# New places in memory for four operand tiles, and a new rank table, in a three-layer fp32 decoder kernel on one core

## The chip, the core and the metric

The kernel runs on one core of a Trainium2 chip as one launch. The metric is the device time of an execution in microseconds (us), as a median of several executions. The engines go by the profile's names: PE is TensorE (PEld its weight loads), DVE is VectorE, ACT is ScalarE, POOL is GpSimd, SP issues the DMAs.

## The reference, cut to what matters

Three transformer layers over 256 tokens of 1024 features, all in fp32: a layer of gated linear attention ("gla"), a layer of sparse attention ("nsa"), both with attention to a memory of 256 rows and a convolutional feed-forward block, and a layer with forgetting attention ("fox"), pooling and 16 meta tokens put ahead.

```python
x = first_block(x, mem, ...)      # for each of two layers:
    h = rmsnorm(x, g_mix[l])
    x = x + gla_layer_mix(h, ...)  or  nsa_layer_mix(h, shared, ...)
    x = x + conv_ffn(rmsnorm(x, g_ffn[l]), w_up[l], conv_w[l], conv_b[l], w_down[l])
return second_block(x, ...)       # _layer: forgetting attention + pooling, then silu(gate) * up, down
```

Nearly all arithmetic is in products of activations with weight matrices of 1024 rows (2816 for the three down projections).

## The kernel before

**Products in three passes.** Every weight piece `w` (128 x up to 1024 numbers) arrives in `wraw` by DMA and is split: ACT rounds it to `whi` (`_cuts`), and DVE subtracts, `wlo = wraw - whi` (`_rest`). Activations are split in the same way into a high and a low tile. A block of 128 output columns is then, for each 128 rows `kk` of the contraction, three matmuls with 128 x 128 stationary weights and 256 streamed columns (`mm3`, line 516 records them): `whi` with the high part, `whi` with the low part, `wlo` with the high part. In the profile's names the weights stand last: `acc<-xh,wlo`.

**Streamed operands.** There are three kinds: the sets `xh`/`xl` (two of them, each 8 x 272 numbers per partition) hold the normed input of a projection; `ch`/`cl` hold the heads' outputs ahead of an output projection; `hh`/`hl` hold the hidden layer ahead of a down projection. All lie in SBUF at addresses that the order of the `base.tile` calls sets. In the built program the pieces `whi` and `wlo` are multiples of 1024 bytes apart. Counted from them modulo 1024 bytes, `ch`, `cl`, `hh` and `hl` lie at 704, both `xl` at 704, and both `xh` at 192. One row `kk` of a streamed operand is 1024 bytes per partition (1088 where it holds 272 columns), one stationary block 512 bytes.

**Order of the work.** The program has no loop. Python generators (threads) yield operations, and `Sched.run` writes the operations out one by one: of the threads that are ready it takes the one with the lowest `cost + NEAR * rank`. The rank comes from the table `PRIO` by the generator's name; `RATIO` and `LIMIT` set a credit that decides when PE's small matmuls may go ahead of a main product. An operation written `V.op | G.op` goes to DVE or POOL, whichever the planner thinks will end it earlier. Engines run their own instructions strictly in the order written, and wait for each other by semaphores.

**The place that the change reorders most** is in the gla layer, for the second half (`tt == 1`) of the tokens. `expo` makes tables on ACT and DVE (`gqe`, `ge`, `gqx`); `levels` multiplies them on PE in groups (`att<-gqe,ge`, `att<-gq,gk`, `att<-gqx,gkx`); `near_pairs` copies each group out of PSUM with DVE (`near<-gc,att`, then `gat<-near` and `gat<-att`); `out_rows` multiplies the result with the values (`att<-gv,gat`, and `att<-gv,gax`). At the same time `mem_set` builds the set for the memory (`xl<-mem,vec,xh`), and `mm3` continues with the projection `mq`.

Of the kernel before, what the change touches and what calls it, by code (L numbers as in the profile page):

```python
# [6 lines left out]
FT = mybir.dt.float32  # L7
FR = mybir.dt.float32r
# [120 lines left out]
class Ev:  # L129


    def __init__(self):
        self.t = None
# [20 lines left out]
class Thread:  # L154
    def __init__(self, gen, prio, t, n):
# [2 lines left out]

LNEXP, EXPTANH, SILU = "natural_log_exp_and_others", "exp_and_others", "silu_and_others"
TABLES = {"Exp": (LNEXP, EXPTANH), "Ln": (LNEXP,), "Silu": (SILU,), "Tanh": (EXPTANH,)}  # L160
LOAD, TICK, RATIO, LIMIT, WARM, SWITCH = 1.3, 3.4133, 1.4792, 0.7664, 12, 0.13
NEAR = 0.00100

PRIO = {"_cuts": -18.58, "_load": 1.02, "_loads": -36.85, "_rest": -3.82, "add_residual": -13.55,
        "both_norms": -19.45, "ck_load": -13.23, "ck_loads": -83.76, "coefs": 59.38, "compress": -19.77,
        "consts": 24.44, "decay": -37.28, "evacuate": 6.42, "expo": -55.79, "few_loads": 48.21, "forget": -38.18,
        "fox_chain": -4.22, "fox_pair": 5.05, "proj_few": 10.05, "fox_head": 2.42, "gains": 32.58, "gate": 23.42,
        "gating": -11.27, "head_norm": -20.5, "heads_of": -2.08, "hidden": 7.95, "late_loads": -16.69,
        "levels": 7.47, "mem_chain": -63.57, "mem_head": -11.75, "meta_probs": 1.9, "meta_rows": 0.62,
        "meta_values": -15.47, "mix": -47.97, "near_pairs": -10.15, "nsa_chain": -4.61, "out_rows": -68.21,  # L170
        "output": -6.62, "pads": 18.74, "pooling": -11.72, "rows_done": 28.61, "rstd_rows": -52.41,
        "scale_few": -6.07, "scale_out": -25.81, "scale_tok": -70.73, "selection": 91.16, "silu": 15.66,
        "smalls": 30.82, "square_sum": -6.06, "squares": 39.11, "stack_k": -9.03, "stack_q": 22.34, "swap": 33.71,
        "tile_parts": -14.4, "up": -47.17, "values": -19.21, "warm": -9.83, ("square_sum", 3): 31.92,
        ("square_sum", 5): 13.26}
HOP = {"P": 0.24, "V": 0.14, "S": 0.16, "G": 0.29, "D": 0.24}


# [222 lines left out]
class Weights:  # L401


    def __init__(self, sch, plan, dram, dma, V, S, G, raw, hi, lo):
        self.sch, self.plan, self.dram, self.dma, self.V, self.S, self.G = sch, plan, dram, dma, V, S, G
# [47 lines left out]

    def _rest(self, p, raw, o, m, left):
        p.lo = yield self.lo
        parts = p.lo[:, :m], raw[:, o:o + m], p.hi[:, :m].bitcast(FT)
        yield self.V.tensor_sub(*parts) | self.G.tensor_sub(*parts)
        self.sch.set(p.ev)
        left[0] -= 1
        if not left[0]:  # L460
            self.sch.give(self.raw, raw)
# [21 lines left out]
def body(tc, io):  # L483
    from contextlib import ExitStack
    nc = tc.nc
    sch = Sched(nc)
    V, S, G = Eng("V", nc.vector), Eng("S", nc.scalar), Eng("G", nc.gpsimd)
# [7 lines left out]
    def slots(pl, n, shape, name, dt=FT):  # L495
        return Slots([pl.tile(shape, dt, name=f"{name}{i}") for i in range(n)])
# [27 lines left out]
    def tr(*calls):  # L524

        def fn():
            for o, a, b in calls:
# [8 lines left out]
    base = pool("base")  # L536
# [6 lines left out]
    W = Weights(sch, _plan(), io["w"], dma, V, S, G, slots(base, 2, [128, CHUNK], "wraw"),  # L543
                slots(base, NP, [128, PIECE], "whi", FR), slots(base, NP, [128, PIECE], "wlo", FR))
    rco = base.tile([128, 10], FT, name="rco")
    rsq = base.tile([128, 10], FT, name="rsq")
    minus_half = base.tile([128, 10], FT, name="mhalf")
    sets = Slots([(base.tile([128, KD, LT], FR, name=f"xh{i}"), base.tile([128, KD, LT], FR, name=f"xl{i}"))
                  for i in range(2)])
    x = base.tile([128, KD, T], FT, name="x")  # L550
    meta = base.tile([128, KD, META], FT, name="meta")
# [5 lines left out]
    tiny = Slots(tinys + [base.tile([128, 32], FT, name=f"tiny{i}") for i in range(2, 10)])  # L557
# [11 lines left out]
    def C(name):  # L569
        o, n = COFF[name]  # L570
        return cst[:, o:o + n]
# [6 lines left out]
        o, n = VOFF[name]  # L578
        return vec[:, o:o + n]

    ident, ones = C("ident"), base.tile([128, 128], FT, name="ones")


    def mm3(ps, b, st, cols=lambda a: a, first=True, last=True):
# [381 lines left out]
    def main():  # L966
# [25 lines left out]
        with ExitStack() as stack:  # L992
# [40 lines left out]
            alrT, qT, kT = t_([128, T], "alrT"), t_([128, 2, T], "gq"), t_([128, 2, T], "gk")  # L1033
# [43 lines left out]
            def expo(tt, f, out):  # L1077
                c = slice(tt * 128, tt * 128 + 128)
                yield la_ev, gr_ev
                et = yield e_  # L1080
                e = et.rearrange("p (a b) -> p a b", a=8)
                qe = yield qes
                for half in range(2):
                    bank = yield att
                    a0 = 128 * tt + 512 * half
                    yield pe(*[(bank, w[:, tt, f * 128:f * 128 + 128], gr[:, a0:a0 + 512], i == 0, i == 1)
                               for i, w in enumerate((lh, ll))])
                    yield S.activation(et[:, half * 512:half * 512 + 512], bank, AF.Exp, scale=1.0 / 16.0)
                    give(att, bank)
                yield q_ev[f], k_ev[f]  # L1090
                l0 = 1 - tt
                yield V.tensor_mul(qe, e[:, l0:l0 + 7], qT[:, f, None, c].to_broadcast([128, 7, 128]))
                ke = e[:, l0:l0 + 7]
                parts = ke, ke, kT[:, f, None, c].to_broadcast([128, 7, 128])
                yield V.tensor_mul(*parts) | G.tensor_mul(*parts)
                if tt == 0:
                    yield V.tensor_mul(kx[:, f, :], e[:, 0], kT[:, f, c])
                else:
                    yield V.tensor_mul(qx[:, f, :], e[:, 7], qT[:, f, c])
                kx_ev[tt, f] = Ev()  # L1100
                sch.set(kx_ev[tt, f])
                out.append((et, qe, ke))
# [458 lines left out]
        rm_ev, c = Ev(), {}  # L1561
# [514 lines left out]
```

## Time and profile before

| | |
|---|---|
| runs shown | 923.35, 929.02, 929.19 us; median 929.02 |
| profiled execution | 923.24 us, of which 921.5 us from the first to the last instruction |
| PE busy | 899.9 us, 7967 matmuls |
| DVE, ACT, POOL busy | 717.0, 493.2, 90.4 us |

PE's busy time counts a matmul from its start to a modelled end, so matmuls that follow each other overlap; how dense PE works is read from the number of matmuls in a stretch. Stages by the span's time: start to 24 us, gla to 101, its output projection to 150.7, first feed-forward block to 327.4, nsa to 420, output projection to 460.6, second feed-forward block to 638, fox to 718.5, output projection to 745, last feed-forward block to the end.

### The profile page before, as it was taken

The page shows a single profiled execution, that of the slowest core. Times are in us where ns is not written, and L with a number is a line of the kernel's source. Part 1 is how long each engine was busy: PE and PEld are TensorE (multiplying, and loading weights), DVE is VectorE, ACT ScalarE, POOL GpSimd, SP SyncE. Part 2 cuts the span into 40 slices and gives each one's busy share as a digit, 9 for nine tenths or more (in the row PEclk, how much of TensorE's full clock was granted, in tenths as well). Part 3 has the DMA queues.
Part 4 walks back from the last instruction along what each step waited for, and adds up shares of the span by engine and source line. Part 5 has one row for each costly group of instructions (what it writes and reads, how often), then busy time and mean ns, then how long its engine had stood idle before and what let it go on. Part 6 is the DMA issues. An engine that isn't in the chain of part 4 may idle for free.

```text
span 921.5 us, 19560 instructions
## 1 busy us (share of the span) xinstructions
PE 899.9 (98%) x7967; PEld 864.7 (94%) x7967; DVE 717.0 (78%) x1492; ACT 493.2 (54%) x854; POOL 90.4 (10%) x116
## 2 busy tenths in 40 slices
PE   8988999999999999999999999999999999999998
PEld 7877999999999996989999999999889999999998
DVE  7776588999987687986899999867688777777552
ACT  5644556555554544875565555545666554444431
POOL 3211001000000012300200000112352100000000
PEclk9977999999999999999999999999999999999999
DMA  7721535555555566233445555555323355555651
GB/s 268 265 70 70 183 138 169 198 183 193 200 202 184 190 239 238 90 138 96 180 184 186 200 206 188 184 186 206 131 93 128 127 182 205 185 187 194 217 209 64
DMA packets 26668, 160.19 MB, mean 174 GB/s; under 512 B 3242, under 2 KB 5674, under 8 KB 8530
## 3 DMA queue, kind: packets, MB, share of 16 engines
q1 hardware_dynamic: 26578, 158.94, 48.5%
q8 instruction: 63, 1.03, 0.4%
q14 instruction: 27, 0.22, 0.1%
HBM read 157.62 MB, written 1.05 MB: 172 GB/s over the span
## 4 chain that ended last, share of the span: by engine, by line
PE 86%; DVE 10%; DMA 2%; issue 1%; ACT 0%; SPq 0%; DVEq 0%; ACTq 0%
PE acc L516 76%; PE att L516 8%; DVE wlo L335 4%; PE att L528 2%; DVE xl L335 2%; DMA ck<-in_w_cv_dram 1%; DVE x L335 1%; DVE sum L335 1%; DMA ck<-in_w_ck_dram 1%; DMA mem<-in_w_dram 0%; DVE xh L335 0%; DVE gqx L335 0%; DVE ge L335 0%; DVE gqe L335 0%; DVE near L335 0%
## 5 line engine op out<-in xcount | busy, mean ns | idle before, releaser
L335 ACT CAST whi<-wraw 128x1024 fp32r<-128x1024 f32 x280 | 294.4, 1052 | 319.5 <-PE acc L516 305.0
L335 DVE TENSOR_TENSOR wlo<-wraw,whi 128x1024 fp32r<-128x1024 f32 x279 | 345.2, 1238 | 103.8 <-ACT whi L335 102.9
L516 PE MATMUL acc<-xh,whi 128*128 128x256 f32 (+1 forms) x1440 | 408.2, 283 | 0.1
L516 PE MATMUL acc<-xh,wlo 128*128 128x256 f32 (+1 forms) x1440 | 400.9, 278 | 2.0 <-DVE wlo L335 2.0
L516 PE MATMUL acc<-xl,whi 128*128 128x256 f32 (+1 forms) x1440 | 401.0, 278 | 1.4 <-DVE xl L335 1.3
L516 PEld LDWEIGHTS acc<-xh,whi 128*128 128x128 f32 x1440 | 271.4, 189 | 6.5 <-issue 4.2
L516 PEld LDWEIGHTS acc<-xl,whi 128*128 128x128 f32 x1440 | 271.9, 189 | 2.6 <-DVE xl L335 2.2
L516 PEld LDWEIGHTS acc<-xh,wlo 128*128 128x128 f32 x1440 | 271.4, 188 | 2.8 <-DVE wlo L335 2.8
L516 PE MATMUL acc<-hh,whi 128*128 128x256 f32 x528 | 146.0, 276 | 0.0
L516 PE MATMUL acc<-hl,whi 128*128 128x256 f32 x528 | 145.7, 276 | 0.0
L516 PE MATMUL acc<-hh,wlo 128*128 128x256 f32 x528 | 145.7, 276 | 0.0
L516 PEld LDWEIGHTS acc<-hh,whi 128*128 128x128 f32 x528 | 99.1, 188 | 0.0
L516 PEld LDWEIGHTS acc<-hl,whi 128*128 128x128 f32 x528 | 99.1, 188 | 0.0
L516 PEld LDWEIGHTS acc<-hh,wlo 128*128 128x128 f32 x528 | 99.1, 188 | 0.0
L335 POOL TENSOR_TENSOR sum<-sum,sqt 128x256 f32<-128x256 f32 x27 | 28.9, 1070 | 477.5 <-ACT sqt L335 469.0
L516 PE MATMUL acc<-ch,whi 128*128 128x256 f32 x192 | 55.3, 288 | 0.0
L516 PE MATMUL acc<-cl,whi 128*128 128x256 f32 x192 | 53.1, 277 | 0.0
L516 PE MATMUL acc<-ch,wlo 128*128 128x256 f32 x192 | 53.1, 277 | 0.0
L335 DVE SCALAR_TENSOR_TENSOR fa<-pad,vec,fa 128x256 f32<-128x256 f32 x88 | 41.7, 478 | 0.0
L335 DVE TENSOR_TENSOR fb<-acc,nb 128x256 f32<-128x256 f32 x66 | 28.0, 424 | 12.4 <-PE acc L516 9.6
L516 PEld LDWEIGHTS acc<-ch,whi 128*128 128x128 f32 x192 | 36.1, 188 | 0.7 <-issue 0.4
L335 DVE TENSOR_TENSOR x<-acc,x 128x256 f32<-128x256 f32 x64 | 26.3, 418 | 12.9 <-PE acc L516 12.6
(337 smaller groups left out, 1044.5 us busy)
## 6 DMA issues: line engine op xcount, KB each, us to landing
wraw<-in_w_dram SPq DMA_DIRECT2D x140, 1024.0 KB, 4.8
ck<-in_w_ck_dram SPq DMA_DIRECT2D x4, 512.0 KB, 5.6
ck<-in_w_cv_dram SPq DMA_DIRECT2D x4, 512.0 KB, 5.5
x<-in_x_dram SPq DMA_DIRECT2D x4, 256.0 KB, 6.0
mem<-in_w_dram SPq DMA_DIRECT2D x4, 256.0 KB, 4.6
mem<-in_mem_dram SPq DMA_DIRECT2D x1, 1024.0 KB, 6.9
out_dram<-sqt SPq DMA_DIRECT2D x8, 128.0 KB, 2.1
ge<-in_gcst_dram SPq DMA_DIRECT2D x2, 288.0 KB, 7.5
```

Of the source, the lines that this page charges most:

```text
L335: op_ = Op(self.name, d, lambda: f(out, *a, **k), table=table)
L516: r = P.matmul(o, a, b, start=s, stop=e)
L528: r = P.transpose(o, a, b)
```

## The change

The change does three things. It puts small tiles between the parts of the two sets, so that `xh0`, `xl0`, `xh1` and `xl1` all lie 704 bytes from the weights modulo 1024: four of the `tiny` tiles (512 bytes) ahead of `xh0`, `meta` (512) after it, `ones` (512) after `xl0`, four more `tiny` after `xh1` (a set's part is 8704 bytes, 512 more than a multiple of 1024). No tile is added. It takes POOL out of the choice for two operations, the split of weights in `_rest` and the product `ke` in `expo`. And it replaces the rank table, `RATIO`, `LIMIT` and `NEAR`.

```diff
-LOAD, TICK, RATIO, LIMIT, WARM, SWITCH = 1.3, 3.4133, 1.4792, 0.7664, 12, 0.13
-NEAR = 0.00100
+LOAD, TICK, RATIO, LIMIT, WARM, SWITCH = 1.3, 3.4133, 1.3862, 1.2333, 12, 0.13
+NEAR = 0.00101
...
-        "levels": 7.47, "mem_chain": -63.57, "mem_head": -11.75, "meta_probs": 1.9, "meta_rows": 0.62,
+        "levels": 0.78, "mem_chain": -69.93, "mem_head": -9.86, "meta_probs": -21.08, "meta_rows": -15.24,
...
-        parts = p.lo[:, :m], raw[:, o:o + m], p.hi[:, :m].bitcast(FT)
-        yield self.V.tensor_sub(*parts) | self.G.tensor_sub(*parts)
+        yield self.V.tensor_sub(p.lo[:, :m], raw[:, o:o + m], p.hi[:, :m].bitcast(FT))
...
-    sets = Slots([(base.tile([128, KD, LT], FR, name=f"xh{i}"), base.tile([128, KD, LT], FR, name=f"xl{i}"))
-                  for i in range(2)])
+    tinys += [base.tile([128, 32], FT, name=f"tiny{i}") for i in range(2, 6)]
+    xh0 = base.tile([128, KD, LT], FR, name="xh0")
+    meta = base.tile([128, KD, META], FT, name="meta")
+    xl0 = base.tile([128, KD, LT], FR, name="xl0")
+    ones = base.tile([128, 128], FT, name="ones")
+    xh1 = base.tile([128, KD, LT], FR, name="xh1")
+    tinys += [base.tile([128, 32], FT, name=f"tiny{i}") for i in range(6, 10)]
+    xl1 = base.tile([128, KD, LT], FR, name="xl1")
+    sets = Slots([(xh0, xl0), (xh1, xl1)])
...
-                parts = ke, ke, kT[:, f, None, c].to_broadcast([128, 7, 128])
-                yield V.tensor_mul(*parts) | G.tensor_mul(*parts)
+                yield V.tensor_mul(ke, ke, kT[:, f, None, c].to_broadcast([128, 7, 128]))
```

On POOL, in the gla stage, one weight split stands between the norm of the memory (`nt`) and the two powers of `out_rows` (`tiny`) before:

```order
19 L335 TENSOR_TENSOR sum_90<-sum_90,sqt_86 128x256
20 L335 TENSOR_TENSOR nt_94<-tiny_64,mhalf 128x2
21 L335 TENSOR_TENSOR wlo_72<-wraw_66,whi_68 128x1024
22 L335 TENSOR_TENSOR tiny_98<-tiny_98,mhalf 128x4
23 L335 TENSOR_TENSOR tiny_99<-tiny_99,mhalf 128x4
```

and now none does; it is the only weight split that POOL had:

```order
19 L335 TENSOR_TENSOR sum_99<-sum_99,sqt_95 128x256
20 L335 TENSOR_TENSOR nt_103<-tiny_64,mhalf 128x2
21 L335 TENSOR_TENSOR tiny_78<-tiny_78,mhalf 128x4
22 L335 TENSOR_TENSOR tiny_79<-tiny_79,mhalf 128x4
23 L335 TENSOR_TENSOR sum_100<-sum_100,sqt_97 128x256
```

On DVE at the same place, before, from the last product of `expo` to the copies of `near_pairs`:

```order
77 L335 TENSOR_TENSOR gqx<-ge_132,gq 128x128
78 L335 TENSOR_TENSOR sr<-acc_113,nb_93 128x256
79 L335 SCALAR_TENSOR_TENSOR xl_81<-mem,vec,xh_80 128x256
80 L335 SCALAR_TENSOR_TENSOR mq<-acc_114,nb_93 128x256
81 L335 SCALAR_TENSOR_TENSOR xl_81<-mem,vec,xh_80 128x256 x7
82 L335 COPY_PREDICATED near<-gc,att_117 128x2x16
83 L335 COPY_PREDICATED near<-gc,att_116 128x2x16
84 L335 TENSOR_TENSOR wlo_73<-wraw_65,whi_69 128x1024
85 L335 COPY_PREDICATED near<-gc,att_117 128x4x8
```

and now:

```order
80 L335 TENSOR_TENSOR gqx<-ge_132,gq 128x128
81 L335 TENSOR_TENSOR sr<-acc_114,nb_102 128x256
82 L335 SCALAR_TENSOR_TENSOR mq<-acc_115,nb_102 128x256
83 L335 SCALAR_TENSOR_TENSOR xl_91<-mem,vec,xh_86 128x256 x8
84 L335 TENSOR_TENSOR wlo_72<-wraw_66,whi_68 128x1024
85 L335 TENSOR_TENSOR wlo_73<-wraw_65,whi_69 128x1024
86 L335 COPY_PREDICATED near<-gc,att_120 128x2x16
```

All eight splits of the memory and two weight splits, one of them the one that POOL had, now stand ahead of the first copy. On PE, before, the twelve products `gv,gat` and `gv,gax` of `out_rows` follow each other without a break, four for the first half of the tokens (bank `att_117`) and eight for the second (`att_116`):

```order
514 L516 MATMUL acc_115<-xl_79,whi_70 128x256
515 L516 MATMUL acc_115<-xh_78,wlo_74 128x256
516 L516 MATMUL att_117<-gv,gat 128x128 x4
517 L516 MATMUL att_116<-gv,gat 128x128
518 L516 MATMUL att_116<-gv,gax 128x128
```

and now nine main matmuls stand between the four products of the first half and those of the second, which need the copies:

```order
516 L515 MATMUL att_119<-gv,gat 128x128 x4
517 L515 MATMUL acc_116<-xh_82,whi_70 128x256
518 L515 MATMUL acc_116<-xl_84,whi_70 128x256
519 L515 MATMUL acc_116<-xh_82,wlo_74 128x256
520 L515 MATMUL acc_116<-xh_82,whi_70 128x256
521 L515 MATMUL acc_116<-xl_84,whi_70 128x256
522 L515 MATMUL acc_116<-xh_82,wlo_74 128x256
523 L515 MATMUL acc_116<-xh_82,whi_70 128x256
524 L515 MATMUL acc_116<-xl_84,whi_70 128x256
525 L515 MATMUL acc_116<-xh_82,wlo_74 128x256
526 L515 MATMUL att_118<-gv,gat 128x128
527 L515 MATMUL att_118<-gv,gax 128x128
```

Over the whole program PE leaves the main products for small ones 122 times before and 120 times now, at nearly the same places; SP's queue differs by one pair of neighbours (`few` ahead of a `wraw`).

## Rows read from the trace of the kernel before

**Rows 1.** The page: span, and busy time, share and instructions of each engine.

```profile
span 921.5 us, 19560 instructions
PE 899.9 (98%) x7967; PEld 864.7 (94%) x7967; DVE 717.0 (78%) x1492; ACT 493.2 (54%) x854; POOL 90.4 (10%) x116
```

**Rows 2.** Two stages: length; PE, PEld, DVE, ACT, POOL busy (count); clock; DMA; GB/s.

```profile
24.00:101.00 77.00, 69.09 (x834) 62.74 (x834) 55.35 (x126) 43.15 (x91) 12.38 (x8) 0.87 0.38 136
...
150.70:327.40 176.70, 176.70 (x1562) 176.70 (x1560) 148.32 (x254) 94.67 (x130) 1.47 (x2) 1.00 0.54 192
```

**Rows 3.** Waits of PE: who for whom, us in total, times, longest.

```profile
PE att L516 <- DVE near L335: 7.9, 4, 4.1
PE acc L516 <- DVE wlo L335: 2.0, 3, 1.1
```

**Rows 4.** Chain that ended last, in order of time: start us, us, what.

```profile
81.53 1.38 PE acc L516 x12
82.90 0.58 PE att L528 x4
83.49 3.77 PE acc L516 x33
...
150.77 176.49 PE acc L516 x1557
...
329.99 2.84 PE acc L516 x24
...
367.70 4.59 PE acc L516 x39
...
436.92 6.49 PE acc L516 x57
```

**Rows 5.** Stretches of main matmuls alone, columns as in rows 2.

```profile
153.00:253.00 100.00, 100.00 (x885) 100.00 (x884) 91.43 (x167) 56.54 (x79) 0.00 (x0) 1.00 0.55 194
...
330.10:342.90 12.80, 12.80 (x111) 12.80 (x110) 12.17 (x26) 7.32 (x11) 1.34 (x3) 1.00 0.86 307
...
383.20:385.40 2.20, 2.20 (x21) 2.20 (x20) 2.20 (x19) 2.20 (x11) 0.10 (x1) 1.00 0.01 4
458.00:460.00 2.00, 2.00 (x19) 2.00 (x19) 0.41 (x2) 0.69 (x1) 0.73 (x1) 1.00 0.98 410
```

**Rows 6.** Timeline of DVE, gla stage: start us, us, what, [idle before, releaser].

```profile
63.95 2.67 DVE L335 TENSOR_TENSOR gqx<-ge,gq 128x128 f32<-128x128 f32 x2
...
67.72 2.85 DVE L335 SCALAR_TENSOR_TENSOR xl<-mem,vec,xh 128x256 fp32r<-128x256 f32 x7
...
70.69 1.22 DVE L335 TENSOR_TENSOR wlo<-wraw,whi 128x1024 fp32r<-128x1024 f32 x1
...
72.73 0.94 DVE L335 COPY_PREDICATED near<-gc,att 128x32 f32<-128x32 uint8 x7 [0.73 <-PE att L516]
74.81 0.36 DVE L335 COPY_PREDICATED near<-gc,att 128x64 f32<-128x64 uint8 x2 [1.14 <-PE att L516]
...
76.32 0.65 DVE L335 COPY gat<-att 64x128 f32<-64x128 f32 x3
```

**Rows 7.** Timeline of the same stretch on POOL and PE.

```profile
63.03 3.24 POOL L335 TENSOR_TENSOR wlo<-wraw,whi 128x1024 fp32r<-128x1024 f32 x1 [10.59 <-ACT whi L335]
...
72.06 0.52 PE L516 MATMUL att<-gq,gk 64*32 64x32 f32 x32 [4.10 <-DVE near L335]
...
77.31 1.91 PE L516 MATMUL att<-gv,gat 128*128 128x128 f32 x8
```

**Rows 8.** Groups by shape, whole span: busy us, mean ns of one.

```profile
L335 DVE TENSOR_TENSOR pu<-acc,rb 128x128 f32<-128x128 f32 x8 | 2.3, 283 | 0.0
```

**Rows 9.** Stretches of the gla stage, columns as in rows 2.

```profile
51.50:60.00 8.50, 8.50 (x81) 7.08 (x82) 4.68 (x17) 3.83 (x9) 0.71 (x1) 0.52 0.01 2
...
67.70:75.80 8.10, 2.98 (x67) 2.30 (x65) 6.20 (x26) 0.56 (x3) 0.00 (x0) 0.64 0.30 123
75.80:83.00 7.20, 7.20 (x46) 7.02 (x45) 2.27 (x10) 5.74 (x22) 1.00 (x1) 0.69 0.00 0
```

More of the change, by code (lines that the diff above doesn't have):

```diff
@@ L160 @@
 TABLES = {"Exp": (LNEXP, EXPTANH), "Ln": (LNEXP,), "Silu": (SILU,), "Tanh": (EXPTANH,)}
-LOAD, TICK, RATIO, LIMIT, WARM, SWITCH = 1.3, 3.4133, 1.4792, 0.7664, 12, 0.13
-NEAR = 0.00100
[L164 to L168, printed above, removed]
-        "levels": 7.47, "mem_chain": -63.57, "mem_head": -11.75, "meta_probs": 1.9, "meta_rows": 0.62,
[L170 to L175, printed above, removed]
@@ new lines @@
+LOAD, TICK, RATIO, LIMIT, WARM, SWITCH = 1.3, 3.4133, 1.3862, 1.2333, 12, 0.13
+NEAR = 0.00101
+PRIO = {"_cuts": -12.17, "_load": 1.37, "_loads": -52.68, "_rest": -5.17, "add_residual": -7.56,
+        "both_norms": -33.22, "ck_load": -15.44, "ck_loads": -83.53, "coefs": 40.79, "compress": -19.2,
+        "consts": 36.87, "decay": -34.57, "evacuate": 4.06, "expo": -64.07, "few_loads": 45.42, "forget": -21.91,
+        "fox_chain": -3.12, "fox_pair": -7.57, "proj_few": 19.88, "fox_head": 8.36, "gains": 38.33, "gate": 50.08,
+        "gating": -14.29, "head_norm": -36.58, "heads_of": -11.63, "hidden": -0.76, "late_loads": -3.72,
+        "levels": 0.78, "mem_chain": -69.93, "mem_head": -9.86, "meta_probs": -21.08, "meta_rows": -15.24,
+        "meta_values": 4.27, "mix": -62.03, "near_pairs": 2.77, "nsa_chain": -9.52, "out_rows": -71.71,
+        "output": -17.96, "pads": 9.38, "pooling": -17.95, "rows_done": 25.04, "rstd_rows": -64.13,
+        "scale_few": -10.36, "scale_out": -20.17, "scale_tok": -36.67, "selection": 77.08, "silu": 5.66,
+        "smalls": 40.36, "square_sum": -10.21, "squares": 50.38, "stack_k": -3.54, "stack_q": 16.96, "swap": 48.72,
+        "tile_parts": -15.56, "up": -32.71, "values": -13.07, "warm": -5.76, ("square_sum", 3): 28.89,
+        ("square_sum", 5): 15.72}
@@ L401, with __init__ @@
 class Weights:
-    def __init__(self, sch, plan, dram, dma, V, S, G, raw, hi, lo):
-        self.sch, self.plan, self.dram, self.dma, self.V, self.S, self.G = sch, plan, dram, dma, V, S, G
+    def __init__(self, sch, plan, dram, dma, V, S, raw, hi, lo):
+        self.sch, self.plan, self.dram, self.dma, self.V, self.S = sch, plan, dram, dma, V, S
         self.raw, self.hi, self.lo = raw, hi, lo
@@ L542, in body @@
     tinys = [base.tile([128, 32], FT, name=f"tiny{i}") for i in range(2)]
-    W = Weights(sch, _plan(), io["w"], dma, V, S, G, slots(base, 2, [128, CHUNK], "wraw"),
+    W = Weights(sch, _plan(), io["w"], dma, V, S, slots(base, 2, [128, CHUNK], "wraw"),
                 slots(base, NP, [128, PIECE], "whi", FR), slots(base, NP, [128, PIECE], "wlo", FR))
@@ L547, in body @@
     minus_half = base.tile([128, 10], FT, name="mhalf")
-    sets = Slots([(base.tile([128, KD, LT], FR, name=f"xh{i}"), base.tile([128, KD, LT], FR, name=f"xl{i}"))
-                  for i in range(2)])
+    tinys += [base.tile([128, 32], FT, name=f"tiny{i}") for i in range(2, 6)]
[7 more added lines that the diff above has]
+    sets = Slots([(xh0, xl0), (xh1, xl1)])
     x = base.tile([128, KD, T], FT, name="x")
-    meta = base.tile([128, KD, META], FT, name="meta")
     vec = base.tile([128, NVEC], FT, name="vec")
@@ L556, in body @@
     norms = Slots([(base.tile([128, 2], FT, name=f"nt{i}"), base.tile([128, T], FT, name=f"nb{i}")) for i in range(3)])
-    tiny = Slots(tinys + [base.tile([128, 32], FT, name=f"tiny{i}") for i in range(2, 10)])
+    tiny = Slots(tinys)
     few, fewg = base.tile([128, 256], FT, name="few"), base.tile([128, KD, 32], FT, name="fewg")
@@ L579, in vcols @@
         return vec[:, o:o + n]
-    ident, ones = C("ident"), base.tile([128, 128], FT, name="ones")
+    ident = C("ident")
     def mm3(ps, b, st, cols=lambda a: a, first=True, last=True):
```

## Prediction

> **What bounds the kernel now.** I read the page first. PE is busy for 899.9 of 921.5 us, DVE for 78% [rows 1], so I looked for PE's time in three places: waits, the clock, and the pace of its matmuls.
>
> The waits are small: 7.9 us in four waits for DVE's copies `near`, 2.0 us for weight splits [rows 3], and then a list of pieces below 2 us. The `near` waits all lie in the gla stage, 24 to 101 us, which is also the one stage with a lowered clock, 0.87 on average against 1.00 in the feed-forward block [rows 2]. After PE had waited for copies, stretches were granted 0.52, 0.64 and 0.69 of full speed: partly its lower level of 1.2 GHz, partly 2.4 GHz [rows 9].
>
> The pace is the part that the page hides. The chain counts 1557 matmuls in 176.49 us from 150.77 us on, 113.4 ns each [rows 4]; these are the first feed-forward block, streamed from `xh`/`xl` and then from `hh`/`hl`. From 329.99 us on it counts 24 in 2.84 us, 118.3 ns, and from 367.70 us on 39 in 4.59 us, 117.7 ns [rows 4], with the same shape and at full clock. So there are two paces, some 4.6 ns apart. In rows 5 the count tells it too (a stretch also counts two or three matmuls that straddle its ends): 885 in 100 us is the fast pace, 111 in 12.8 us and 21 in 2.2 us are the slow one. What goes with the slow pace? Not DVE: it is busy 91% of a fast stretch, and 0.41 of 2.00 us in a slow one (458 us). Not the DMAs: their share is 0.86 and 0.98 in two slow stretches and 0.01 in a third [rows 5]. A stream seems to fall into one pace after an interruption and to keep it until the next. What does separate them is the tile: I find the slow pace for long only in streams from `xh`/`xl`; `ch`/`cl`, which lie at 704, run 57 in 6.49 us, 113.9 ns [rows 4], and `hh`/`hl` at 704 are fast throughout. `xh` is the one part at 192.
>
> **The change part by part.** All sums start from the profiled execution, 923.24 us (its span of 921.5 and 1.74 around it). It equals the fastest run shown, 923.35; the median, 929.02, is 5.8 us above it, and two of three runs lie there.
>
> *Spacers.* They add no instruction. If the offset of 192 is what lets a stream fall into the slow pace, all `xh`/`xl` streams now run at 113.4 ns. Slow in this profile were, counted start to start in streams of eight or more: 111, 39, 21 and 19 in the stretches at 330, 367, 383 and 458 us [rows 4, 5], 190 in all, and by my count some 160 more in shorter streams of the same kind. 350 x 4.6 ns = 1.6 us. The upper end is every `xh`/`xl` matmul outside the three up projections (some 860 of 4032), 4.0 us; the lower end is nothing. I take 1.6. There is more in it than this sum: an up projection is one stream of about 1000 matmuls, and all three were fast in this profile. One that falls into the slow pace costs 1000 x 4.6 ns = 4.6 us, which is nearly the step between the two levels of the runs shown (5.7 us). If that is what they are, the spacers also take away the upper level.
>
> The Trainium skill speaks against all of this: "TensorE: Matmul & The Clock Gate", section "Step-by-step: what each phase is for", says that PE reads streamed operand and weights through two independent ports, so that a weight load takes nothing from the matmul that runs. By that rule the address of `xh` is worth 0 and this term falls out of the sum. The trace has two paces where that rule, as it stands, has one, but it doesn't show that the address makes them; I keep it as a rival.
>
> *POOL out of two choices.* `ke` was on DVE already, so that edit moves nothing. The weight split was on POOL once, 3.24 us at 63.03 [rows 7], and is now one more on DVE, 1.22 us [rows 6]. While it ran, DVE's two products `gqx` of 128x128 took 2.67 us [rows 6]; DVE operations of that size take 283 ns elsewhere [rows 8]. I take the difference, 2.67 - 0.57 = 2.1 us, as given back on DVE.
>
> *New order in gla, second half of the tokens.* Before, PE stands at `gq,gk` from 67.97 to 72.06 [rows 7]: that group is written behind DVE's first copies, shares their PSUM banks and waits for them, and they stand behind seven splits `xl` (2.85 us) and a weight split [rows 6]. Now PE's groups are all written ahead of the copies, so this wait goes. What is late next is `out_rows` of the second half, which needs the last copy. DVE's way there: before, from the end of `gqx` at 66.62 to the end of the last copy at 76.97, 10.35 us, in which DVE itself waited for PE for 0.73 and 1.14 us [rows 6]. Now: `gqx` ends at 66.62 - 2.1 = 64.5, then 10.35 - 1.87 + 1.22 (the second weight split) + 0.2 (one copy more), 9.9 us, so the last copy ends at 74.4. PE, without its stop, is there by about 70.5: `gq,gk`, the rest of the groups, nine main matmuls ahead and nine behind the first `gv,gat`, each a microsecond or less. It then stands for 4 us, in another place. What is gained is what it has done by then: before, `gv,gat` begins at 77.31 [rows 7]; now, at 74.4, nine more main matmuls and the first four of the twelve products are done. The other eight are sixteen rows of the profile; at the lower clock's 0.21 us (8 rows in 1.91 us) they take 3.4 us, to 77.8. Before, the same point lies nine main matmuls behind 81.53 [rows 4], at about 82.5: 4.7 us earlier. Against that stands the clock. Before, the lowered clock fell mostly on PE's own stop (0.64 in 67.7 to 75.8), and 7.2 x 0.31 = 2.2 us of it on work [rows 9]. Now the stop begins 2.5 us later, and as much more of the lowered clock falls on dense work: another 2.2 us lost. Net 2.5 us gained. Bounds: 4.7 if the clock isn't lowered; a loss of 1.2 if POOL's split gave DVE nothing and the second split is simply added. Everything behind this place is PE's own work without long waits, so the gain lasts to the end.
>
> *Other places.* One switch from main to small matmuls and back costs 0.19 us: 45 main matmuls and four transposes from 81.53 to 87.26 us take 5.73 us, against 45 x 113.4 ns and 4 x 0.11 [rows 4]. Two switches fewer give 0.4 us. In nsa and fox the same operations stand a few matmuls from their old places; PE waits little there and I price this at 0, with 2.5 us to either side, about the size of the second entry of rows 3. `few` passes one weight load in SP's queue: 0.
>
> The sum: 923.24 - 1.6 - 2.5 - 0.4 = **918.7 us**, 1.1% below the median before.
>
> **The rivals.**
>
> *The spacers do nothing, and the levels stay.* For it: the rule above, and that two thirds of the `xh`/`xl` stream ran fast at 192. Then the lower level is 923.24 - 2.9 = 920.3 and the upper 926.0. Against it: no long slow stream from a tile at 704.
>
> *The upper level of the runs is a clock, not a pace.* One more stop with a lowered clock behind it, say at the nsa stage's waits for DMAs, costs what 51.5 to 60 us shows: 8.5 x 0.48 = 4.1 us [rows 9]. The spacers then leave it, and the median of after is on either level: 918.7 or about 924.5. For it: 5.7 us is more than the 4.6 of one slow stream.
>
> *Slower: 704 for both parts is the wrong pair.* If the pace hangs on how high and low part lie to each other, and `xh` at 192 was what kept the up projections fast, three streams of 1000 now fall into the slow pace: 3 x 4.6 = 13.8 us more, 923.24 - 2.9 + 13.8 = 934.1. It decides when one whole up projection shows 118 ns. Against it: `ch`/`cl` and `hh`/`hl` have both parts at 704 and are fast.
>
> **How the numbers follow.** Differences of about 1% (9.3 us) are what a measurement of this kernel can tell from no change. The forecast's own range is 915.5 to 922 with a chance of 0.48; no effect of the spacers (920.3 or 926) 0.15; a clock that stays (924.5) 0.22; the slower pair 0.06; unpriced shifts in nsa and fox beyond 2.5 us 0.09. The bounds of gla (from 4.7 gained to 1.2 lost) and of the pace (4.0 to 0) reach from 914 to 924 on the lower level, and the upper level lies 4 to 5.7 above. The range that leaves out two tenths is 913 to 927.5. More than 1% faster than 929.02 means below 919.7: about two thirds of the forecast and bits of the others, 0.36. Within 1%: 0.58. Slower than 938.3: 0.06.
>
> **What would show it.** Right: no stream of main matmuls longer than eight at 117 ns or more from `xh`/`xl`; no wait of `gq,gk` for `near` in the second half, and a wait of about 4 us of `gv,gat` instead; `gqx` at 0.3 us each; runs on one level. Wrong: slow streams from tiles at 704; a `near` wait as long as before; a lowered clock in another stage; or two levels of runs again.

## The result, and the profile after

The change takes the median from 929.19 us (9 runs, 922.55 to 936.71) to 920.67 us (9 runs, 913.71 to 922.83); the measured ratio is 0.9886, interval 0.9857 to 0.9915 (the two medians alone give 0.991). The forecast was 918.7 in a range of 913 to 927.5. That the number is so near is luck: at an equal pace of the feed-forward blocks the change gains twice what was forecast, and most runs of after lose even more than that surplus in one slow block, which the forecast had ruled out.

The profiled execution of after took 920.78 us. First its page: the span, and the busy time of each engine.

```profile
span 919.0 us, 19557 instructions
PE 902.6 (98%) x7967; PEld 869.4 (95%) x7967; DVE 716.4 (78%) x1502; ACT 489.8 (53%) x844; POOL 87.1 (9%) x116
```

The span is 2.5 us shorter than in [rows 1] and PE is busy 2.7 us longer. The chain of the work that ended last says why (start us, us, what):

```profile
143.44 183.38 PE acc L515 x1557
...
329.56 13.07 PE acc L515 x111
...
458.83 133.29 PE acc L515 x1176
...
742.62 173.10 PE acc L515 x1527
```

Against [rows 4]: the first feed-forward block begins 7.3 us earlier (143.44 for 150.77), and its 1557 matmuls take 183.38 us in place of 176.49. That is 117.8 ns each in place of 113.4: the whole block, `hh` and `hl` included, ran at the slow pace, with every streamed part at 704. The second and third block run at 113.3. So 7.3 us are gained up to there and 6.9 of them are lost again in one block.

Stretches of gla and of that block (length; PE, PEld, DVE, ACT, POOL busy with counts; clock; DMA; GB/s) answer to [rows 2, 5, 9]:

```profile
24.00:101.00 77.00, 72.95 (x879) 66.38 (x878) 59.54 (x137) 44.11 (x89) 7.91 (x7) 0.96 0.45 158
...
153.00:253.00 100.00, 100.00 (x851) 100.00 (x851) 88.42 (x161) 51.93 (x73) 0.00 (x0) 1.00 0.53 187
...
67.70:75.80 8.10, 7.40 (x100) 6.95 (x100) 7.18 (x29) 3.69 (x17) 0.00 (x0) 1.00 0.34 131
75.80:83.00 7.20, 7.20 (x64) 7.20 (x63) 4.13 (x7) 5.24 (x13) 1.98 (x2) 1.00 0.43 148
```

In gla the clock is 0.96 on average where it was 0.87, and from 67.7 to 83 us it is 1.00 where it was 0.64 and 0.69. In the block, 851 matmuls stand in 100 us where 885 stood, at a clock of 1.00: the pace is not the clock.

PE's waits (who for whom, us in total, times, longest), against [rows 3]:

```profile
PE att L515 <- DVE near L335: 2.1, 2, 1.8
...
PE att L515 <- DVE gat L335: 0.7, 1, 0.7
```

And the timeline of gla's second half on DVE and on PE (start us, us, what, idle before and its releaser), against [rows 6, 7]:

```profile
63.24 0.48 DVE L335 TENSOR_TENSOR gqx<-ge,gq 128x128 f32<-128x128 f32 x2
...
69.74 1.55 DVE L335 COPY_PREDICATED near<-gc,att 128x32 f32<-128x32 uint8 x12
71.20 1.22 DVE L335 COPY gat<-near 32x64 f32<-32x64 f32 x8
72.44 0.78 DVE L335 COPY gat<-att 64x128 f32<-64x128 f32 x4
...
67.73 0.36 PE L515 MATMUL att<-gq,gk 64*32 64x32 f32 x19 [0.87 <-issue]
...
70.44 1.05 PE L515 MATMUL att<-gv,gat 128*128 128x128 f32 x8
...
73.23 0.46 PE L515 MATMUL att<-gv,gat 128*128 128x128 f32 x2 [0.68 <-DVE gat L335]
```

`gqx` takes 0.24 us each where it took 1.33. The twelve `near` copies run in one piece, without a wait for PE; the last copy ends at 73.2, where it ended at 76.97. PE no longer stops at `gq,gk` for 4.10 us; it has 0.87 us without work in the middle of that group (`<-issue`: the profile shows nothing that it waited for), and 0.68 us ahead of `gv,gat`.

**Levels.** All runs of before that were taken beside the experiments, 100 with those above, lie in groups: 42 near 923.2, 47 near 929.4, 8 near 934.9, 3 near 940.3 (medians; the upper groups are less sharp). The step, 5.3 to 6.2 us, is about what one feed-forward block costs at the slow pace: 6.9 us for the first, 5.2 for the second (138.50 for 133.3 us, below), 7.0 for the third (180.06 for 173.10). So I read the groups as 0, 1, 2 or 3 slow blocks; in all 11 profiles of whole kernels the group of the run and the number of slow blocks in its trace agree. The clock doesn't make the groups: over a whole run it is 0.990 on average in the lowest group and in the next (91 runs that list it). After has 2 runs near 914.0 and 7 near 920.7. At an equal number of slow blocks the change gains 9.2 and 8.7 us, three times the 2.9 that the sum had for it apart from the spacers.

In what follows one stretch serves as a ruler, because it leaves out the start and the feed-forward blocks: from the 211th matmul of 128x256 into `acc` to the 601st, counted in each trace (63.85 to 145.40 us before). It takes 81.55 us before and 74.95 after.

### The profile page after: what moved, and what is told of

It is laid out like the page before. It is cut to its first block, busy times and chain, and to the rows that moved or that the text cites. A ratio compares the mean times of both kernels' runs of the same rounds, so it can differ in the third digit from the quotient of the medians.

```text
span 919.0 us, 19557 instructions
## 1 busy us (share of the span) xinstructions
PE 902.6 (98%) x7967; PEld 869.4 (95%) x7967; DVE 716.4 (78%) x1502; ACT 489.8 (53%) x844; POOL 87.1 (9%) x116
## 4 chain that ended last, share of the span: by engine, by line
PE 88%; DVE 8%; DMA 2%; issue 1%; ACT 0%; SPq 0%; DVEq 0%; ACTq 0%
PE acc L515 79%; PE att L515 7%; DVE wlo L335 3%; PE att L527 2%; DVE xl L335 2%; DMA ck<-in_w_cv_dram 1%; DVE x L335 1%; DMA x<-in_x_dram 1%; DVE sum L335 0%; DMA ck<-in_w_ck_dram 0%; DVE ge L335 0%; DVE gqe L335 0%; DVE xh L335 0%; SPq L499 0%; ACT whi L335 0%
## 5 line engine op out<-in xcount | busy, mean ns | idle before, releaser
L515 PEld LDWEIGHTS acc<-cl,whi 128*128 128x128 f32 x192 | 36.1, 188 | 0.3
```

The source lines that it names most:

```text
L515: r = P.matmul(o, a, b, start=s, stop=e)
```

## The experiments

**1. Streams alone (e1).** Does the address make the pace? A kernel of the three products of a weight tile, in streams behind several kinds of restart, at several offsets; DVE, ACT and DMA do next to nothing.

```diff
+VARIANTS = ((192, 704, 0), (704, 704, 0), (0, 0, 0), (192, 704, 1))   # offsets of xh, xl; order of the products
+KINDS = ("nt", "nf", "f1", "f2", "dve")                               # what stands ahead of a stream
...
+        for oh, ol, order in VARIANTS:
+            for kind in KINDS:
+                for r in range(REPS):
+                    restart(kind, r)
+                    stream(17 + r, oh, ol, order, wx if kind == "dve" else whi)
```

> A kernel of matmul streams alone; it leaves out the whole computation of the reference and keeps the kernel's pair of weight parts and streamed parts with the three products in the kernel's order. Four variants of ten streams (51 to 78 matmuls of 128x256) behind each of five kinds of restart: two 128x128 transposes (as ahead of the feed-forward blocks), the same and one plain fp32 128x256 matmul, one such matmul, two of them, a wait for a DVE copy of the weights. Variants: streamed parts at 192 and 704 modulo 1024 from the weights, at 704 and 704, at 0 and 0, and at 192 and 704 with the two products of one streamed part side by side. If the address makes the pace: slow streams (near 118 ns) at 192/704 and none at 704/704, behind every kind of restart. If the restart chooses it: the same share of slow streams at 192/704 and 704/704, some 3 in 10 behind the transposes and near none behind the fp32 128x256 matmuls. If it takes the other engines' traffic: no slow stream at all, 113.4 ns everywhere.

Chain of this kernel: at 192 and 704 a stream behind the transposes and two behind one fp32 matmul; then at 704 and 704 the same three; then one at 0 and 0.

```profile
27.02 6.49 PE acc L524 x57
...
170.18 6.01 PE acc L524 x51
...
190.55 6.81 PE acc L524 x60
...
425.88 6.49 PE acc L524 x57
...
569.03 6.01 PE acc L524 x51
...
589.41 6.81 PE acc L524 x60
...
989.15 6.83 PE acc L524 x57
```

6.49 us for 57 and 6.81 for 60 are the fast pace, 6.01 for 51 is the slow one. Start to start, without each stream's beginning, there are two values and nothing between them: 113.3 and 117.8 ns. At 192/704 and at 704/704 the count is the same: 8 of 10 slow behind one fp32 matmul, 1 of 10 behind two, none behind the transposes and one fp32 matmul or a wait for DVE, none behind the transposes alone (leaving out the very first stream, which began at 213 ns a matmul and went over to 113 at 17 us). So both paces exist without traffic of other engines, and the spacers' step from 192 to 704 changes nothing. At 0/0 all streams run at 120.0 ns: the address does matter, but not these two. The order of the products doesn't matter much either (9 of 50 slow at 192/704, 10 of 50 with the other order). So the address expectation fails, and the shares of the restarts are the other way round than the second one had them: none slow behind the transposes, most behind the fp32 matmul.

**2. The spacers alone (e2), and the change without them (e3).** The instructions of every engine stand in the order of before in e2, of after in e3.

```diff
e2, on before:
-    sets = Slots([(base.tile([128, KD, LT], FR, name=f"xh{i}"), base.tile([128, KD, LT], FR, name=f"xl{i}"))
-                  for i in range(2)])
+    xh0 = base.tile([128, KD, LT], FR, name="xh0")
+    meta = base.tile([128, KD, META], FT, name="meta")
+    xl0 = base.tile([128, KD, LT], FR, name="xl0")
...
e3, on after: the same lines the other way round
```

> Before with the spacers alone; the instructions stand in the same order on every engine. If the address makes the slow pace (the prediction's theory): all runs near 921.5 us, no stream above eight at 118 ns. If a whole feed-forward block falls into a pace at its start, whatever the address (now the first theory): runs stay on levels 6.9 us apart, near 923, 930 and 937, median within 0.2% of before, slow streams from tiles at 704 in the trace.

> After without the spacers: new ranks and the smaller choice for GpSimd, streamed parts at 192 and 704 as before; the order of instructions is that of after. If the spacers bring part of the gain: 923 to 929 us. If they bring nothing: runs on the levels of after, near 914 and 921, ratio 0.986 to 0.992.

e2: ratio 1.0014 (0.9983 to 1.0045); 4, 7 and 1 runs in the groups. e3: 914.7 us median, ratio 0.9897 (0.9861 to 0.9932); 5 runs near 913.4, 3 near 919.9. The ruler says 81.60 for e2 and 75.2 for e3. So no part of the gain comes from the spacers. That e3 has more runs in the lowest group than after (5 of 8 for 2 of 9) is too few runs to read anything from.

**3. POOL out of the choices alone (e4).** Old ranks, old layout; one weight split comes back to DVE.

```diff
-        yield self.V.tensor_sub(*parts) | self.G.tensor_sub(*parts)
+        yield self.V.tensor_sub(p.lo[:, :m], raw[:, o:o + m], p.hi[:, :m].bitcast(FT))
...
-                yield V.tensor_mul(*parts) | G.tensor_mul(*parts)
+                yield V.tensor_mul(ke, ke, kT[:, f, None, c].to_broadcast([128, 7, 128]))
```

> Before with GpSimd taken out of the two choices alone, old ranks. Only one weight split moves from POOL to DVE and four small copies to ACT. If the two instructions on one port cost DVE 2.1 us and that is the gain: the gla stage ends 2 to 7 us earlier, levels near 917 and 924. If the order of PE's groups is what matters: PE's wait of 4.1 us stays (3 to 5 us) and with it the lowered clock behind it, the stage ends within 1.5 us of before, levels 922 and 929.

Timeline of e4 on DVE and PE:

```profile
62.33 0.48 DVE L335 TENSOR_TENSOR gqx<-ge,gq 128x128 f32<-128x128 f32 x2
...
68.26 0.41 PE L515 MATMUL att<-gq,gk 64*32 64x32 f32 x32 [1.90 <-DVE near L335]
```

`gqx` is short and PE's stop shrinks from 4.10 to 1.90 us, by the 2.1 us that the prediction had DVE win. The ruler gives 79.21, 2.3 us less than before; the lowest group lies at 920.3 (923.2). The ratio over all runs, 1.0004 (0.9967 to 1.0040), shows none of this, since the draw of slow blocks covers it. Neither expectation met it: the stop is halved, not kept, and half of it isn't all of the gain.

**4. The new ranks with POOL left in (e7).** After, with the two alternatives put back.

```diff
-        yield self.V.tensor_sub(p.lo[:, :m], raw[:, o:o + m], p.hi[:, :m].bitcast(FT))
+        yield self.V.tensor_sub(*parts) | self.G.tensor_sub(*parts)
...
-                yield V.tensor_mul(ke, ke, kT[:, f, None, c].to_broadcast([128, 7, 128]))
+                yield V.tensor_mul(*parts) | G.tensor_mul(*parts)
```

> After with GpSimd put back into the two choices: a weight split returns to POOL in the gla stage and some small copies change engine with it. If the order of PE's groups alone makes the gain (ranks): the first feed-forward stream begins within 1 us of after's 143.4, levels near 914.5 and 921. If DVE's slow-down under POOL's split is a part of its own, as the prediction has it (2.1 us): the copies end 1 to 3 us later, a PE wait for them of 2 to 4 us returns, and with it a lowered clock: 917 to 920 on the lower level.

Timeline of before on DVE, one line, then of e7 on DVE, POOL and PE:

```profile
61.95 2.09 DVE L335 TENSOR_TENSOR ge<-ge,gk 128x896 f32<-128x896 f32 x2
...
59.99 4.29 DVE L335 TENSOR_TENSOR ge<-ge,gk 128x896 f32<-128x896 f32 x2
...
60.90 2.42 POOL L335 TENSOR_TENSOR wlo<-wraw,whi 128x1024 fp32r<-128x1024 f32 x1 [9.05 <-ACT whi L335]
...
69.95 0.47 PE L516 MATMUL att<-gq,gk 64*32 64x32 f32 x19 [2.09 <-issue]
```

The scheduler puts the split on POOL a little earlier, and now another pair of DVE operations pays: two products `ge` take 4.29 us where they took 2.09 before. The tax is 2.2 us again, as with `gqx`: the pair ends at 64.28, one product's 1.0 us behind the end of POOL's split at 63.32, so the second one has stood still until then. (The Trainium skill, "SBUF — State Buffer", "SBUF: two separate sides", says this of a DVE operation with two SBUF inputs beside a GpSimd operation that reads SBUF: one has the shared ports for its whole length, the other blocks. These rows agree, with 2.2 us for the second `ge`.) PE loses 1.48 us waiting for `ge` and 2.09 us inside `gq,gk`, and the clock from 60 to 101 us is 0.88. The 2.09 us are no wait for the copies, which was the wait expected back; they fall between the same two matmuls as after's 0.87 us. The ruler gives 80.32: of the gain of 6.6 us only 1.2 is left. The lowest group is at 918.5, the median 925.51, ratio 0.9974 (0.9938 to 1.0010). The planner also writes PE's operations behind the stop in another order than in after (the twelve `gv,gat` and `gv,gax` follow each other again), so this isn't the ranks alone in every place.

**5. PE kept at work through its stop (e6, e10).** Is it the stop or the lowered clock behind it? Before, with plain fp32 matmuls of 128x128, result unused, ahead of `gq,gk`.

```diff
+                        if (tt, lv) == (1, 7):
+                            fn, op.fn = op.fn, lambda fn=op.fn: (fill(36), fn())     # e10: fill(18)
```

> Before with 36 plain fp32 matmuls of 128x128 (about 3.9 us, result not used) written ahead of the group of gq,gk at which PE stands for 4.1 us in the second half of gla, so that PE works through its wait. Nothing else moves. If the lowered clock behind the stop is a good part of what the new order gained (half to two thirds of 7 us): the clock stays at 1.00 from 70 to 80 us, the first feed-forward stream begins 3 to 4.5 us earlier than before's 150.7, levels near 919 and 926. If the stop itself was all of it: 923 and 929, the stream at 150.7; if the fillers are longer than the stop, later than that.

> Before with 18 fillers in place of 36: the first count was sized at 0.11 us each and each took 0.228 (8.20 us for 36), 4 us longer than the stop. 18 take 4.1 us, as long as PE's stop. From the 211th to the 601st main matmul before takes 81.55 us and after 74.95. If the lowered clock is the larger part of what the new order gained there: 76.5 to 78.5, clock 1.00 from 66 to 84 us. If the stop is the larger part: 79.5 to 81, the clock at 1.00 all the same, and waits behind it in place of the slow work.

The first was mis-sized: each filler shows as two matmuls in the trace, and 36 took 8.20 us, so this kernel is 2.9 us slower on the ruler (84.40), ratio 1.0058. The second fits. Its timeline on PE, and the stretch from 60 to 101 us of before and of e10:

```profile
67.58 4.18 PE L1130 MATMUL acc<-ones 128*128 128x128 f32 x36
...
81.48 0.63 PE L528 MATMUL att<-cst,lt 128*128 128x128 f32 x4 [1.71 <-DVE lt L335]
```

```profile
60.00:101.00 41.00, 35.88 (x465) 34.04 (x464) 30.18 (x73) 23.23 (x56) 6.16 (x3) 0.88 0.24 83
...
60.00:101.00 41.00, 38.19 (x512) 36.56 (x511) 31.17 (x73) 23.28 (x57) 6.17 (x3) 1.00 0.28 97
```

With PE busy through the wait the clock stays at 1.00 (0.88 before in this stretch). The ruler gives 80.43, only 1.1 us less: a new wait of 1.71 us for `lt` stands at the next place, where PE used to arrive late. That is the second expectation. The ratio is 0.9996 (0.9959 to 1.0033). So in before's order much of what the clock costs is hidden by the work that leads to `lt`: copies on DVE, sums on ACT, a power on POOL, a product on DVE.

**6. The first half too (e8).** After with 16 such fillers at its wait of 1.75 us in the first half (the lines of experiment 5 with `(0, 5)` and `fill(16)`), and with the fp32 matmul of experiment 7.

> After with the fp32 matmul ahead of the three feed-forward streams and with 16 plain fp32 matmuls of 128x128 (1.7 us) ahead of the fourth group of gqe,ge in the first half of gla, where PE waits 1.75 us for near. If PE's stop brings the lowered clock there too: the clock stays at 1.00 from 49 to 58 us and 2 to 3 us more are gained: all runs between 911 and 914. If not: the same as with the fp32 matmul alone, 913 to 916.

Stretches of e8, and a line of its timeline on PE:

```profile
52.00:55.00 3.00, 3.00 (x71) 2.63 (x72) 1.25 (x10) 0.79 (x2) 0.71 (x1) 1.00 0.02 5
...
70.00:76.00 6.00, 6.00 (x36) 6.00 (x36) 3.00 (x18) 2.60 (x11) 0.00 (x0) 0.64 0.37 153
...
66.41 0.33 PE L515 MATMUL att<-gqe,ge 64*32 64x16 f32 x16 [1.44 <-issue]
```

The clock stays up in the first half, as expected (0.50 in after at that place, the lower level of 1.2 GHz). But PE then stands 1.44 us inside a group of `gqe,ge`, with no releaser that the profile shows, and the clock falls in the second half, to 0.64 from 70 to 76 us. The ruler gives 77.67, 2.7 us worse than after; the lowest group is at 916.0, the ratio 0.9939 (0.9899 to 0.9979). Nothing was gained: a lowered clock was moved.

This stop and after's in `gq,gk` are the same one. In after, e3, e5, e7, e8 and e12 it always stands behind the same count of PE's instructions in the trace, 731 matmuls and 732 weight loads; in e8 the 32 matmuls of the fillers are among them, so that `gqe,ge` falls there. Each time the trace's DMA records have a load of 16 KB on the queue named `instruction`, begun 2.2 to 2.6 us before PE goes on (65.38 and 67.73 us in after). So PE probably waits for its own program there; no run tested it.

**7. Can a restart be made that leaves the blocks fast (e5, e12)?** After, with one fp32 matmul more between the two transposes and each feed-forward block.

```diff
         yield tr(...)                                          # the two transposes of bcast_tok
...
+        P.matmul(bank[:, 256:512], ones, vec[:, 0:256], start=True, stop=True)             # e5
+        P.matmul(bank[:, 256:272], ones[0:16, :], ones[0:16, 0:16], start=True, stop=True) # e12
```

> After with one more plain fp32 matmul of 128x256 right behind the two transposes that stand ahead of each feed-forward block's long stream (three in all, about 0.22 us each); its result is not used and the order of everything else is that of after. In the kernel of streams alone 40 of 40 streams behind this sequence ran at 113.3 ns. If the pace is chosen at the restart and the two levels of the runs are paces of these blocks: no run near 921, all between 913 and 916, all three blocks fast in the trace, ratio to before near 0.985. If the upper level is a clock or anything that happens inside a block: runs on two levels as with after, 914.5 and 921.5.

> After with one plain fp32 matmul of 16 rows by 16 columns (about 0.3 us, result not used) in place of the 128x256 one, right behind the two transposes ahead of each feed-forward stream. In all ten profiles of whole kernels the stream behind two such small matmuls in the second feed-forward block is fast, also in the three in which the block was slow up to there. In the same profiles a block whose lead of 19 matmuls was fast started fast each time, one whose lead was slow started slow in about a third. If it is the kind of restart that takes a slow stream to the fast pace: all three blocks fast, no run near 921, all between 913.5 and 916. If the phase at the restart decides and the kind does not: slow blocks in the trace or runs near 921 as with after, ratio to before near 0.99 either way.

Neither does it. e5 has 1, 6 and 5 runs near 915.1, 921.3 and 927.8; e12 has 3, 6 and 3 near 915.0, 921.4 and 928.5. Chain of e5 (its second block, slow up to an interruption), and chain of e12 (its third block, slow):

```profile
453.60 138.50 PE acc L515 x1176
```

```profile
736.09 180.06 PE acc L515 x1527
```

The ratios of the two, 0.9966 (0.9928 to 1.0003) and 0.9897 (0.9857 to 0.9937), differ by how many blocks of their runs, and of before's beside them, happened to be slow. My theory that the kind of restart decides is refuted for these two kinds. The expectation of e5 also misread e1: behind that sequence 30 of 40 streams ran at 113.3 ns, and the ten at 0/0 ran at 120.0.

**8. Which offsets have a fast pace (e9, e11)?** Streams alone, behind one fp32 matmul of 128x256.

```diff
-VARIANTS = ((192, 704, 0), (704, 704, 0), (0, 0, 0), (192, 704, 1))
+VARIANTS = tuple((o, o, 0) for o in range(0, 512, 32))                                          # e9
+VARIANTS = tuple((o, o, 0) for o in range(164, 224, 4)) + (pairs with one part at 192)          # e11, the pairs in words
...
```

> Streams alone again; the computation of the reference is left out. Both streamed parts at one offset from the weights, 0 to 480 in steps of 32 (the weights step by 512, so offsets 512 apart meet the same pairs), each with eight streams behind one plain fp32 matmul of 128x256, which made 7 of 10 streams slow at 192/704 and at 704/704, and eight behind the two transposes. If the offset decides which paces there are (at 0 every stream ran at 120.0 ns, a third pace): some offsets show one pace only, and if one of them shows 113.3 ns alone, that layout takes the upper levels of the runs away. If 192 modulo 512 is the best there is: the others show 120 ns or both paces. If the offset is without effect but for 0: all others show 113.3 and 117.8 in the share of the first such kernel, 0.7 behind the fp32 matmul.

> Streams alone, each behind one plain fp32 matmul of 128x256; the computation of the reference is left out. Both streamed parts at one offset from the weights, 164 to 220 in steps of 4, and then one part at 192 while the other takes 0, 32, 64, 96, 128, 160 or 224, eight streams each. The sweep in steps of 32 showed 113.3 and 117.8 ns at 64 and 192 modulo 256 alone and slower paces everywhere else. If 192 is the middle of a good region: a few offsets beside it show 113.3 ns alone, and a layout there takes the upper levels of the runs away. If 192 is as good as any: the neighbours show paces between 113.3 and 120 with none that is all fast. If only the offset of the part multiplied twice counts, pairs with the high part at 192 show 113.3 and 117.8 whatever the low part's, and the others not.

Chain of e9, one stream each at 0, 32, 64, 128, then two at 192 and one at 224:

```profile
67.55 8.62 PE acc L524 x72
...
189.43 8.40 PE acc L524 x72
...
257.45 5.78 PE acc L524 x51
...
554.63 8.54 PE acc L524 x72
...
773.11 7.15 PE acc L524 x63
797.46 8.48 PE acc L524 x72
...
918.79 8.51 PE acc L524 x72
```

By starts the paces are 120.0 ns at 0, 116.7 or 117.8 at 32, 113.3 or 117.8 at 64, 120 at 96, 118.7 or 120 at 128, 117.3 to 120 at 160, 113.3 or 117.8 at 192, 118.3 at 224; from 256 to 480 the same eight come again. So of sixteen offsets four have the fast pace at all, 64 and 192 modulo 256, and all four have the slow one too. (The 7 of 10 that the expectation of e9 quotes from e1 are 8 of 10.) In e11 no neighbour of 192 from 164 to 220 shows 113.3 (116.7 to 123.3), nor does any pair with one part elsewhere, 192 with 64 included. Chain of e11: at 188, at 192 (two), at 196, and at 192 with 64.

```profile
441.44 8.48 PE acc L524 x72
...
478.02 7.15 PE acc L524 x63
...
502.36 7.66 PE acc L524 x65
...
565.40 8.75 PE acc L524 x72
...
1124.05 8.48 PE acc L524 x72
```

Before's 192 and after's 704 are the same place modulo 256 (704 = 2 x 256 + 192). That explains why the spacers do nothing: the layout before was already in the good class, and that class has two paces.

## Why the prediction was right in its number and wrong in two terms

**The two paces.** Right: they exist, 4.5 ns apart, are not the clock, and a stream keeps its pace until an interruption. Wrong: "What does separate them is the tile". It was a pattern of one profile. `hh`/`hl` were fast there because the blocks that they end were fast; after has 528 such matmuls in a row at the slow pace, and the step from 192 to 704 has no part in it (e1, e2, e3). The term of 1.6 us is 0. The rival that the spacers do nothing is confirmed in its outcome.

The Trainium skill's reason for that rival ("TensorE: Matmul & The Clock Gate", "Step-by-step: what each phase is for": operand and weights come through independent ports) isn't confirmed: as the prediction read it the offset would be without effect, and e9 and e11 show 113.3 to 123.3 ns by the offset of the streamed operand from the weights, with DVE, ACT and DMA idle. What in the chip makes these paces is not shown.

**The levels.** Right: a level is the pace of a feed-forward block and not a clock. Mis-sized: the stream is not the up projection's 1000 but the whole block's 1557 of [rows 4], so a slow one costs 6.9 us and not 4.6. That misfit (5.7 us seen against 4.6) was what spoke for the rival with the clock, and it was an error in the count. Wrong: that the spacers take the upper level away. With 7 of 9 runs of after on it, the median is 920.67 and not 914. So the near hit is luck: at an equal level the forecast had 4.5 us of gain where the groups show 9.2, and the slow block takes 6.7 us of it back (920.7 for 914.0).

**Gla.** This is the term that was mis-sized most: 2.5 us forecast, with 4.7 as its upper end; the ruler shows 6.6 (81.55 to 74.95), and over before and e2 against after, e3, e5 and e12 (74.7 to 75.6) it is about 6.5. POOL's share was right: 2.1 us on DVE forecast, 2.2 seen in e4's stop and in e7's two `ge`. The step that failed is the next: "It then stands for 4 us, in another place", and with it "as much more of the lowered clock falls on dense work". PE stands 0.68 us there. The copies are done 1.2 us earlier than forecast (73.2 for 74.4): `gqx` ends at 63.72 where 64.5 was forecast, and the way from there takes 9.5 us in place of 9.9. PE comes 1.8 us later (its last matmul ahead of the wait starts at 72.27). The products behind the wait, 3.4 us in the forecast at the lower clock, take 2.02 us at 1.00 (73.23 to 75.25), so the point that was to be reached at 77.8 is reached at 75.25. The 2.2 us that the forecast took off for dense work at a lowered clock behind it aren't lost either: the clock stays at 1.00. The two halves of the change are not additive: 2.3 us for POOL alone (e4), 1.2 for the ranks alone (e7), 6.6 together, since with either one alone PE still stops for about 2 us in the middle of this work (1.90 for the copies in e4; 1.48 for `ge` and 2.09 for no wait that the profile shows in e7), and the clock is lowered behind it (0.96 and 0.88 from 60 to 101 us). With both it is 1.00 in after, e3 and e12. In e5 it is 0.96 and the ruler still shows 75.60: there PE comes late enough that no wait for the copies is left ahead of `gv,gat`. So the clock alone isn't the gain.

Summed over the ruler, the traces give the size of each part. PE's gaps above 0.15 us fall from 5.55 us before to 1.97 after. The time in which PE worked at half the clock falls from 7.1 us to none; at half speed that is an estimate of 3.6 us. So about half of the 6.6 us is waiting and half is the clock, and the forecast had both of them come back at another place. This says where the time went, not what each part would give alone (e10).

**Other places.** 0.4 us forecast, 2.0 seen, inside the 2.5 that were allowed: from the end of the first block to the second's long stream 132.0 us for 133.4, from the second block's end to the third's long stream 106.5 for 107.1 (from the chains). Which operation brings it wasn't tried. The first half of gla also gains, 0.9 us from the 121st to the 211th main matmul (22.8 on average over before, e2, e4, e6 and e10, 21.8 over after, e3, e5, e7 and e12), with as much scatter between profiles of one order. 6.5 + 0.9 + 2.0 is 9.4, against 9.2 between the lowest groups.

**The other rivals.** The slower pair (934.1) didn't come: a whole block did show 118 ns, the sign named for it, but the old layout shows it as often: by the groups 0.72 slow blocks a run in the 100 runs of before, 0.75 in the 12 of e2. The clock as the source of the levels is out, at 1.00 in a slow block.

**Open.** What sets a block's pace at its start. In the 11 profiles of whole kernels each long stream of a block has a lead of some 20 matmuls ahead of the two transposes. Where the lead was fast, the block was fast, 13 of 13; where it was slow, 7 of 20 were slow. In the kernels of streams alone most streams behind the transposes stay in the pace of the one ahead (fast ten times at 704/704 in e1, slow eight times at 192 in e9). So a pace is carried across a short interruption, and only some interruptions end it; their kind doesn't tell which (e5, e12). The exact instant of the restart may. In the traces, six of the 20 slow leads begin with 115 or 119 ns between their first two matmuls, and all six blocks behind them are slow; 14 begin with 117 or 118 ns, and one of their blocks is slow. That pattern was found afterwards in few cases, and no run tested it.

## What to carry to other kernels

When the runs of a kernel lie in groups, find what a step is (here one block of 1557 matmuls at 117.8 in place of 113.3 ns) and compare kernels group by group: a median can hide a gain of 9 us behind one slow block of 7. A property that separates two kinds of streams in one profile can be chance; a kernel of streams alone costs one run and settles it. A stop of PE can cost twice, once as a wait and once as a lowered clock behind it, so two edits that each shorten it may do little alone and much together.

## What the runs showed of the hardware

- Dense fp32r matmuls of 128x256 with a weight load each have discrete paces set by the offset of the streamed operand from the weights: 113.3 ns only where both parts lie at 64 or both at 192 modulo 256 among the offsets tried, 116.7 to 123.3 elsewhere (e1, e9, e11), and four bytes beside 192 cost 4 to 8%. In the good places there are two stable paces, 113.3 and 117.8; in the slow one, every third weight load lasts 192 ns in place of 188 (after's first block).
- One 128x1024 `tensor_tensor` on POOL holds up DVE's two-input product beside it by 2.2 us at both sizes seen: two of 128x896 take 4.29 us in place of 2.09 (e7), two of 128x128 take 2.67 in place of 0.48 (before).
- PE stands 0.67 to 2.09 us in the middle of a group of 32 small matmuls in after, e3, e5, e7, e8 and e12, each time behind 731 matmuls and 732 weight loads, and goes on 2.2 to 2.6 us after a 16 KB load on the queue `instruction` began. That it waits for its program is likely and not tested.
- Plain fp32 matmuls of 128x128 keep the clock at 1.00 through a wait: 18 of them, 4.18 us, in e10.
